# A hybrid decoder step on one core: gates and values projected 512 columns at a time, and the stores at the attention's ends issued by GpSimd

## The chip, the cores and the metric

The kernel runs on one core of one Trainium2 chip. The metric is the device time of one execution in microseconds (us); three runs of the kernel before gave a median of 3208.82 us, from 3206.28 to 3214.18. Engines are called as the profile calls them: PE (TensorE), PEld (its weight loads), DVE (VectorE), ACT (ScalarE), POOL (GpSimd) and SP (SyncE, which here only issues DMAs). Each engine works through its own instructions in order; an instruction that waits holds up everything behind it on that engine, DMA issues included.

## The reference, cut to what matters

One layer of a decoder with two kinds of heads, for one new sequence of 2048 tokens (the prompt) and 64 sampled tokens that attend to a paged cache. All is float32.

```python
z = einsum('bsd,dc->bsc', x, w_in)        # input projection, 1024 -> 3600 columns
fq, fk, fv, flogf = ...                   # 8 attention heads of 64: queries, keys, values, forget gates
mq, mk, mv, ig, lf = ...                  # 4 mLSTM heads of 128 (q and k through a short convolution)
og = sigmoid(z[..., OFF_M_O:] + b_og)     # output gate, 512 columns
fox_h = softmax(q k^T / 8 + decay, causal) v            # prompt attention, 2048 x 2048 per head
(C, n, m), m_h = scan of mLSTM chunks                   # states C_prompt, n_prompt are outputs
mn  = normalise(m_h) * mlstm_norm_w * og
x1  = layer_norm(ALPHA * x + concat(fox_h, mn) @ w_o)
y   = layer_norm(ALPHA * x1 + square(relu(x1 @ w1)) @ w2)
```

The sampled tokens take the same path, with attention over 8192 cached positions each.

## The kernel before, in words

Every large product is split: each float32 operand is taken as a high part (fp32r, made by ACT in `split_hi`, L153) and a rest (made by DVE in `split_lo`, L156), and `mm3` (L162 to L164) does three matmuls in place of one: high by high, and the two mixed ones.

**Phase A, the input projection**, goes over the prompt in four blocks of four 128-token tiles (block 1 has the sampled tokens as a fifth tile). `block_a` runs, for each block: the mLSTM values (two passes of 256 columns, the second with 16 gate columns), eight passes of 128 columns for the convolved q and k, two passes of 256 columns for the output gates, eight of 128 for queries and keys, and two of 256 for the attention's values, which are stored to `v_prompt`. In the passes of 128 columns the weights are the stationary operand and 512 tokens stream past. In the passes of 256 columns (`natural`) a token tile is stationary and 256 weight columns stream past: for each of the four tiles 8 row groups of 128 by 3 matmuls into one PSUM bank, then the pass's `sink` evacuates that bank. `wload` brings the weights of a pass in two pieces of 512 KB (four row groups by 256 columns, two raw buffers `wra`, four split ones `whi` and `wlo`).

Beside the projection run two other streams, a piece at a time: `tick` adds up microseconds and, whenever a pace is passed, issues one step of the mLSTM recurrence (`m_block`, one step per 2.3) or of the sampled tokens' attention (`sample_attention`, one step per 5.6). In `natural` a tick of 2.6 follows each tile. A step of the sampled attention has 32 small matmuls on gathered keys (`sQ`), or 16 on gathered values (`sO`); POOL issues the gathers (`kT`, `vt`). The sampled attention stops at a fixed step in phase A and goes on in later phases.

**Phase B**, the prompt's attention, is 64 units of (head, 256 queries), with the scores `pS` one unit ahead of the values `po`. Before a score leaves PSUM (DVE, L989 and L993), it needs the row of decays `nl` from DRAM and its masked last tile `nd`, which POOL makes (L974). At the end of each half of a head, `finish` scales the output `ot` by `rl` and stores it to the buffer `dmix` (L1061, L1062).

**Phase O** multiplies `dmix` by `w_o` (`pw`, with `mh`, `ml` from `dmix` and `wh`, `wl` from `w_o`, here in passes of 512 columns), and **phase C** is the MLP with one level of Strassen's scheme (`ph`, `py`).

The order of instructions on each engine is fixed when the program is built, by a scheduler that simulates the engines; the buffers (`bufs=`) limit how far ahead it may go.

Of the kernel before, what the change touches and what calls it, by code (L numbers as in the profile page):

```python
# [10 lines left out]
F32 = mybir.dt.float32  # L11
F32R = mybir.dt.float32r
I32 = mybir.dt.int32
AF = mybir.ActivationFunctionType
# [38 lines left out]
def body(ctx, tc, I, O, stages):  # L53
# [411 lines left out]
    def block_a(bi):  # L465
# [3 lines left out]
        def natural(sink, *cols, hook=None, after=None):  # L469
            wh, wl = W0.pop() if W0 else wload(*cols)  # L470
            for i, t in enumerate(blk):
# [9 lines left out]
                    after(i)  # L481
                tick(2.6)

        def stage(ps, m, n):
            st = pa.tile([128, 256], F32, name="st", bufs=4)[:m, :n]
            A.copy(st, ps)
            return st
# [68 lines left out]
        if bi == 3:  # L556
            SY.dma_start(O["conv_prompt"], hist)
        yield 1
        for i in range(2):
# [41 lines left out]
        for i in range(2):  # L601
            def sink(t, m, ps, i=i):
                d = v_out(t)[:, i * 256:(i + 1) * 256]
                (A if bi == 3 and i == 1 else SY).dma_start(d, stage(ps, m, 256))
# [9 lines left out]
            def b_first(n, i=i):  # L614
                if i == 1 and n == 0:
                    begin_b()
            natural(sink, (1024 + i * 256, 256), hook=b_first if bi == 3 else turn_first)

    dgs_s = drm.tile([4, 8], F32, name="dgs_s")

# [5 lines left out]
    def norm_out(hh, np_, og, tok0, eng=None):  # L626

        st = pm.tile([128, 4, 6], F32, name="st6", bufs=2)
        mv = pm.tile([128, 4, 2], F32, name="mv2", bufs=2)
        for h in range(4):  # L630
            V.bn_stats(st[:np_, h], hh[:, h])
            V.bn_aggr(mv[:np_, h], st[:np_, h])
        r = pm.tile([128, 2, 4], F32, name="r4", bufs=2)
        V.tensor_scalar(r[:np_, 0], mv[:np_, :, 1], EPS, None, op0=OP.add)
        G.tensor_tensor(r[:np_, 1], r[:np_, 0], nhalf[:np_, 0:4], op=OP.pow)
        for h in range(4):
            V.tensor_scalar(hh[:, h], hh[:, h], mv[:np_, h, 0:1], r[:np_, 1, h:h + 1], op0=OP.subtract, op1=OP.mult)
        hf = hh.rearrange("p h e -> p (h e)")
        (eng or G).tensor_tensor(hf, hf, og, op=OP.mult)

        def turn():
            po = ppm.tile([128, 4, 128], F32, name="mm", tag="mm", bufs=2)
            for h in range(4):
                T.transpose(po[:, h, :np_], hh[:, h], ident[:np_, :np_])
            ot = pm.tile([128, 4, 128], F32, name="ot", bufs=1)
            A.copy(ot[:, :, :np_], po[:, :, :np_])
            SY.dma_start(dmv[:, 4:8, tok0:tok0 + np_], ot[:, :, :np_])
        mst["turn"] = turn

    def turn_out():  # L650
# [28 lines left out]
    def m_block(bi):  # L679

        if bi == 0:
            mst["C"] = pm.tile([128, 4, 129], F32, name="Cs", bufs=2)
            V.memset(mst["C"], 0.0)
        gsb = pm.tile([128, 4, 4], F32, name="gsb", bufs=2)
        va, Wm, qa = m_load(bi * 4, mst["gates"])
        SY.dma_start(gsb, dap(dgs, bi * 4, [[0, 128], [16, 4], [1, 4]]))
        for _ in range(4):
            yield 1
        A.activation(gsb, gsb, AF.Exp)
        for c in range(bi * 4, bi * 4 + 4):  # L690
# [24 lines left out]
            pk = ppm.tile([128, 4, 128], F32, name="mm", tag="mm", bufs=2)  # L715
            for h in range(4):
                T.transpose(pk[:, h], qk[:, 4 + h], ident)
            kw = pm.tile([128, 4, 128], F32, name="kw", bufs=1)
            for h in range(4):
                V.tensor_scalar(kw[:, h], pk[:, h], wk[:, h:h + 1], KSC, op0=OP.mult, op1=OP.mult)  # L720
            hh = pm.tile([128, 4, 128], F32, name="hh", bufs=1)
            for p in range(2):
                yield 1
                pn = ppm.tile([128, 2, 129], F32, name="mn", tag="mm", bufs=2)
                for i in range(2):
                    h = 2 * p + i
                    T.matmul(pn[:, i], Wm[:, h], va[:, h], start=True, stop=False)
                    T.matmul(pn[:, i], qa[:, h], Cs[:, h], start=False, stop=True)
                h_out(pn, 2 * p, den[:, 2 * p:2 * p + 2], 128, hh)
            Cn = pm.tile([128, 4, 129], F32, name="Cs", bufs=2)  # L730
            va_ = va
            for p in range(2):
                yield 1
                pc = ppm.tile([128, 2, 129], F32, name="mn", tag="mm", bufs=2)
                for i in range(2):
                    T.matmul(pc[:, i], kw[:, 2 * p + i], va_[:, 2 * p + i], start=True, stop=True)
                for i in range(2):
                    h = 2 * p + i
                    V.scalar_tensor_tensor(Cn[:, h], Cs[:, h], gsb[:, h, c % 4:c % 4 + 1], pc[:, i], op0=OP.mult, op1=OP.add)
                if p == 0:  # L740
                    norm_out(hh, 128, og, t0, V if c == 15 else None)
                    if c % 4 < 3:
                        va, Wm, qa = m_load(c + 1)
            mst["C"] = Cn
        mst["open"] = False
        if bi < 3:
            return
        Cs = mst["C"]
        SY.dma_start(O["C_prompt"][0, 0].rearrange("h d e -> d h e"), Cs[:, :, 0:128])
        nn = pm.tile([128, 4], F32, name="nn", tag="sm", bufs=1)  # L750
        V.tensor_copy(nn, Cs[:, :, 128])
        SY.dma_start(O["n_prompt"], nn)
        yield 1
        turn_out()

# [148 lines left out]
    def phase_b():  # L904
# [95 lines left out]
        def values(z, g, sc):  # L1000
# [40 lines left out]
            A.copy(od, po[0:64])  # L1041
            q0 = 128 if g == 0 else 0
            V.tensor_tensor(od[:, q0:], od[:, q0:], po[64:128, q0:], op=OP.add)
            if g % 4 == 3:
# [2 lines left out]
        def finish(z, half):  # L1047
# [9 lines left out]
            for q in range(2):  # L1057
                rl = pb.tile([64, 512], F32, name="rl", bufs=2)
                SY.dma_start(rl, dap(drl, h * S + o + q * 512, [[0, 64], [1, 512]]))
                s = slice(q * 512, (q + 1) * 512)  # L1060
                G.tensor_tensor(ot[:, s], ot[:, s], rl, op=OP.mult)  # L1061
                SY.dma_start(dmix[h // 2, (h % 2) * 64:(h % 2) * 64 + 64, o + q * 512:o + q * 512 + 512], ot[:, s])  # L1062

        kns = [pb.tile([128, 512], F32, name="kn", bufs=3)]
        homes = {}
# [17 lines left out]
        for n in range(len(units) + LA):  # L1083
# [3 lines left out]
            while n and len(w2_done) < min(60 if False else 64, w2_due[0]):  # L1087
                w2_sum()
            if n == 60:
                wo.extend(half_wo(0, q) for q in range(4))  # L1090
            if n < len(units):
                h, g = units[n]
                sc[n] = scores(Z[h], g)
# [916 lines left out]
```

## Time and profile before

| | |
|---|---|
| median of three runs (lowest to highest) | 3208.82 us (3206.28 to 3214.18) |
| the profiled execution's own time | 3212.34 us |
| its span, first to last instruction | 3210.6 us |
| PE busy | 3115.6 us (97%) in 20445 matmuls |
| DVE / ACT / POOL busy | 2080.9 (65%) / 1442.2 (45%) / 902.6 us (28%) |
| mean granted TensorE clock | 0.989 |
| DMA | 732.67 MB, mean 228 GB/s |

Phase A ends at about 867 us of the span, phase B at about 1310, phase O at about 1545. A matmul's duration in the profile is its way through a pipeline: the next one starts before it ends. What a matmul costs a stream of matmuls is the distance from its start to the next one's start.

### The profile page before, as it was taken

To read this page: it belongs to the slowest core of one execution; us is meant where nothing else is said; L and a number is where in the kernel's file an instruction comes from. 1 tells how busy PE (TensorE), PEld (TensorE's weight loads), DVE (VectorE), ACT (ScalarE), POOL (GpSimd) and SP (SyncE) were. 2 spreads that over 40 slices of the span, in tenths; PEclk is the share of its full clock that TensorE was granted. 3 is DMA by queue.
4 is the path that set the end of the run, shared out by engine and by line. 5 is a ranking of instruction groups with operands and counts; after the bars stand their busy time and mean duration, and the time that the engine had idled before them with its cause. 6 is when DMAs were issued, how large, how long until landed. Compare 5 with 4: busy or idle time off the path is not lost. (4 is left out here: it accounts for less than half of the span.)

```text
span 3210.6 us, 55049 instructions
## 1 busy us (share of the span) xinstructions
PE 3115.6 (97%) x20445; PEld 2475.3 (77%) x20445; DVE 2080.9 (65%) x5046; ACT 1442.2 (45%) x2654; POOL 902.6 (28%) x973
## 2 busy tenths in 40 slices
PE   8999999999899999999999999999999999899998
PEld 8997797888767667777677777777767777698886
DVE  6957556465488788534557568556675665766667
ACT  3343343333277777412444445343444444344442
POOL 0121223423333333376333323334333111000000
PEclk9999999999999999999999999999999999999999
DMA  5565766866777865687887869878879866643231
GB/s 190 156 216 179 253 210 211 295 238 228 238 241 189 204 170 138 223 295 257 300 289 269 308 234 322 319 260 307 292 260 340 288 209 204 211 165 131 98 126 63
DMA packets 325075, 732.67 MB, mean 228 GB/s; under 512 B 63592, under 2 KB 161384, under 8 KB 323912
## 3 DMA queue, kind: packets, MB, share of 16 engines
q1 hardware_dynamic: 237672, 414.67, 39.8%
q0 software_dynamic: 83520, 304.12, 27.3%
q10 hardware_dynamic: 3616, 10.36, 0.9%
q8 instruction: 162, 2.65, 0.3%
q14 instruction: 105, 0.86, 0.1%
HBM read 676.20 MB, written 86.38 MB: 238 GB/s over the span
## 5 line engine op out<-in xcount | busy, mean ns | idle before, releaser
L156 DVE TENSOR_TENSOR wl<-wr,wh 128x1024 fp32r<-128x1024 f32 x300 | 365.9, 1223 | 244.0 <-ACT wh L153 204.8
L153 ACT ACTIVATE wh<-wr 128x1024 fp32r<-128x1024 f32 x300 | 315.3, 1055 | 332.0 <-PE py L164 123.7
L162 PE MATMUL ph<-x1h,wh 128*128 128x512 f32 (+1 forms) x1280 | 455.4, 356 | 0.0
L163 PE MATMUL ph<-x1l,wh 128*128 128x512 f32 (+1 forms) x1280 | 453.7, 355 | 0.2 <-DVE x1l L156 0.2
L164 PE MATMUL ph<-x1h,wl 128*128 128x512 f32 (+1 forms) x1280 | 451.7, 355 | 0.2
L1727 POOL DMA_INDIRECT kT<-cache_k,idxK x256 | 277.0, 1082 | 551.9 <-PE sQ L1750 483.2
L162 PE MATMUL py<-wh,hh 128*128 128x512 f32 x900 | 358.9, 403 | 10.1 <-issue 3.6
L163 PE MATMUL py<-wl,hh 128*128 128x512 f32 x900 | 354.5, 395 | 0.2 <-issue 0.2
L164 PE MATMUL py<-wh,hl 128*128 128x512 f32 x900 | 351.8, 395 | 0.4 <-DVE hl L156 0.4
L1376 DVE TENSOR_TENSOR y<-y,py 128x512 f32<-128x512 f32 x410 | 277.2, 683 | 108.4 <-PE py L164 83.0
L1838 POOL DMA_INDIRECT vt<-cache_v,idxV x164 | 178.9, 1091 | 401.4 <-PE sO L1862 341.5
L162 PEld LDWEIGHTS ph<-x1h,wh 128*128 128x128 f32 x1280 | 241.4, 189 | 40.6 <-issue 8.2
L164 PEld LDWEIGHTS ph<-x1h,wl 128*128 128x128 f32 x1280 | 240.8, 189 | 36.5 <-issue 3.7
L163 PEld LDWEIGHTS ph<-x1l,wh 128*128 128x128 f32 x1280 | 241.5, 189 | 34.9 <-issue 3.7
L162 PE MATMUL pm<-whi,xh 128*128 128x256 f32 (+2 forms) x816 | 238.2, 292 | 8.0 <-ACT whi L153 7.9
L163 PE MATMUL pm<-wlo,xh 128*128 128x256 f32 (+2 forms) x816 | 233.9, 287 | 1.0 <-DVE wlo L156 0.6
L164 PE MATMUL pm<-whi,xl 128*128 128x256 f32 (+2 forms) x816 | 234.1, 287 | 0.0
L162 PE MATMUL pm<-xh,whi 128*128 128x512 f32 (+2 forms) x640 | 230.5, 360 | 0.0
L164 PE MATMUL pm<-xh,wlo 128*128 128x512 f32 (+2 forms) x640 | 227.4, 355 | 0.0
L163 PE MATMUL pm<-xl,whi 128*128 128x512 f32 (+2 forms) x640 | 226.8, 354 | 0.0
L162 PEld LDWEIGHTS py<-wh,hh 128*128 128x128 f32 x900 | 169.3, 189 | 66.1 <-issue 25.8
L164 PEld LDWEIGHTS py<-wh,hl 128*128 128x128 f32 x900 | 170.7, 190 | 40.3 <-issue 2.3
(364 smaller groups left out, 6545.2 us busy)
## 6 DMA issues: line engine op xcount, KB each, us to landing
wr<-w SPq DMA_DIRECT2D x200, 512.0 KB
wra<-w_in SPq DMA_DIRECT2D x104, 512.0 KB
wr<-dw SPq DMA_DIRECT2D x96, 512.0 KB
dw<-w POOLq DMA_DIRECT2D x48, 512.0 KB
Rb<-dR SPq DMA_DIRECT2D x128, 128.0 KB
kT<-dw SPq DMA_DIRECT2D x28, 512.0 KB
kT<-w SPq DMA_DIRECT2D x25, 512.0 KB
xn<-xp_t SPq DMA_DIRECT2D x16, 512.0 KB
```

Source lines behind the costliest of these rows:

```text
L153: last["ACT"] = A.activation(dst, src, AF.Copy, scale=scale)
L156: r = (eng or V).tensor_tensor(dst, src, hi.bitcast(F32), op=OP.subtract)
L162: T.matmul(ps, wh, xh, start=first, stop=False, skip_group_check=shared)
L163: T.matmul(ps, wh, xl, start=False, stop=False, skip_group_check=shared)
L164: last["PE"] = T.matmul(ps, wl, xh, start=False, stop=stop, skip_group_check=shared)
L1376: V.tensor_tensor(y, y, ps, op=op)
L1727: G.indirect_dma_start(out=piece(n), out_offset=None, in_=ck, in_offset=IO(ap=idxK[:, b, j // 2, j % 2:j % 2 + 1], axis=0))
L1838: vx["last"] = G.indirect_dma_start(out=vt.rearrange("p f c -> p (f c)"), out_offset=None, in_=cv, in_offset=IO(ap=idxV[:, b, (kt % 4) * 4 ...
```

## The change

Three things change.

**Wider passes.** In blocks 2 to 4 the two passes of the output gates, and the two of the attention's values, become one pass of 512 columns each (`wide`). Four PSUM banks are open at once, one for each tile, and the weights come in four pieces of two row groups by 512 columns (still 512 KB, now read as two runs of 2 KB per partition in place of one of 4 KB). Each piece serves all four tiles before the next begins; a tile's bank is evacuated in the last piece, in one instruction where there were two, and stored in one DMA of 256 KB. The tick is 1.3 after each tile of each piece, and 1.23 for the sampled attention. The loads and the split of the next block's tokens hang on pieces of the values pass (`at`). Block 1 keeps its passes.

**Stores moved to GpSimd.** At the end of phase A, the last mLSTM tile's store to `dmix`, `C_prompt` and `n_prompt` are issued by POOL in place of SP. In block 4 all stores of the values are issued by ACT.

**The end of phase B.** For the last head's second half the scaling by `rl` goes from POOL to DVE and its stores from SP to POOL; the last unit's copy out of PSUM goes from ACT to DVE; and a fifth piece of `w_o` is loaded early.

```diff
+        def wide(sink, c0, hook=None):
+            banks = [ppa.tile([128, 512], F32, name="pm", tag="pm", bufs=4) for _ in blk]
+            at0, at1 = (w_at[((c0 + i * 256, 256),)] for i in range(2))
+            for q in range(4):
+                wr = pa.tile([128, 4 * 272], F32, name="wra", bufs=2)[:, :1024]
+                SY.dma_start(wr.rearrange("p (s e) -> p s e", s=2),
+                             dap(I["w_in"], at0 + q // 2 * 131072 + q % 2 * 512, [[1024, 128], [at1 - at0, 2], [1, 512]]))
...
+                split_hi(wh, wr)
+                split_lo(wl, wr, wh)
...
+                for i, t in enumerate(blk):
+                    xh, xl = xcol(bi, t)
+                    for k in range(2):
+                        mm3(banks[i].rearrange("p (s c) -> p s c", s=2), xh[:, 2 * q + k], xl[:, 2 * q + k], wh[:, k], wl[:, k],
+                            q == k == 0, q == 3 and k == 1)
+                    if hook:
+                        hook(q, i)
+                    if q == 3:
...
+                        sink(t, banks[i], st)
+                    tick(1.3, 1.23)
...
+        if bi:
+            wide(gate_out, C_O)
+        for i in range(0 if bi else 2):
...
+        def v_store(t, ps, st):
+            A.copy(st, ps)
+            (A if bi == 3 else SY).dma_start(v_out(t), st)
...
+        if bi:
+            wide(v_store, 1024, at)
+        for i in range(0 if bi else 2):
...
-            SY.dma_start(dmv[:, 4:8, tok0:tok0 + np_], ot[:, :, :np_])
+            (G if tok0 == S - 128 else SY).dma_start(dmv[:, 4:8, tok0:tok0 + np_], ot[:, :, :np_])
...
-        SY.dma_start(O["C_prompt"][0, 0].rearrange("h d e -> d h e"), Cs[:, :, 0:128])
+        G.dma_start(O["C_prompt"][0, 0].rearrange("h d e -> d h e"), Cs[:, :, 0:128])
...
-        SY.dma_start(O["n_prompt"], nn)
+        G.dma_start(O["n_prompt"], nn)
...
-            A.copy(od, po[0:64])
+            if (z["h"], g) == units[-1]:
+                V.tensor_copy(od, po[0:64])
+            else:
+                A.copy(od, po[0:64])
...
-                G.tensor_tensor(ot[:, s], ot[:, s], rl, op=OP.mult)
-                SY.dma_start(dmix[h // 2, (h % 2) * 64:(h % 2) * 64 + 64, o + q * 512:o + q * 512 + 512], ot[:, s])
+                end = (h, half) == (7, 1)
+                (V if end else G).tensor_tensor(ot[:, s], ot[:, s], rl, op=OP.mult)
+                (G if end else SY).dma_start(dmix[h // 2, (h % 2) * 64:(h % 2) * 64 + 64, o + q * 512:o + q * 512 + 512], ot[:, s])
...
-                wo.extend(half_wo(0, q) for q in range(4))
+                wo.extend(half_wo(*q) for q in ((0, 0), (0, 1), (0, 2), (0, 3), (1, 0)))
```

**Where instructions stand now.** Rows are `line operation out<-in size`, the line being that of each kernel's own source. First SP, at the passage from phase A to phase B, before the change: `Rb` is a load for the sampled attention, `nl0` the first decays of phase B, `vn0` and `kn` its values and keys.

```order
L647 DMA dmix_67<-ot_9777 128x4x128
L1734 DMA Rb_16283<-dR_69 128x1x256 x2
L749 DMA C_prompt<-Cs_9878 128x4x128
L752 DMA n_prompt<-nn_9970 128x4
L647 DMA dmix_67<-ot_9978 128x4x128
L932 DMA nl0_10000<-dnl_64 128x512
L933 DMA vn0_9999<-v_prompt 128x4x64
```

The same place on SP after the change.

```order
L226 DMA kn0_9072<-k_prompt 64x512
L226 DMA qn0_9073<-dq_60 64x256
L694 DMA dmix_67<-ot_9089 128x4x128
L979 DMA nl0_9304<-dnl_64 128x512
L980 DMA vn0_9303<-v_prompt 128x4x64
```

The load of `nl0` no longer stands behind the three last stores of the mLSTM, but behind the store of the last tile but one. POOL at the same passage before the change: `vt` are the two halves of a gather of cached values, `dmask` the causal mask.

```order
L635 TENSOR_TENSOR r4_9956<-r4_9956,nhalf_74 128x4
L1838 DMA vt_9909<-cache_v,idxV_1539 128x1024
L1838 DMA vt_9911<-cache_v,idxV_1539 128x1024
L926 MEMSET ls_10007 128x32
L926 MEMSET ls_10197 128x32
L1078 AFFINE_SELECT dmask_10009<-dmask_10009 128x128
L974 TENSOR_TENSOR nd_10021<-nl0_10000,dmask_10009 128x128
```

POOL at the same passage after the change.

```order
L682 TENSOR_TENSOR r4_9208<-r4_9208,nhalf_74 128x4
L796 DMA C_prompt<-Cs_9174 128x4x128
L799 DMA n_prompt<-nn_9240 128x4
L973 MEMSET ls_9311 128x32
L973 MEMSET ls_9501 128x32
L1889 DMA vt_9281<-cache_v,idxV_1539 128x1024
L1129 AFFINE_SELECT dmask_9313<-dmask_9313 128x128
L694 DMA dmix_67<-ot_9248 128x4x128
L1889 DMA vt_9283<-cache_v,idxV_1539 128x1024
L1021 TENSOR_TENSOR nd_9325<-nl0_9304,dmask_9313 128x128
```

Three stores and the two halves of the gather now stand ahead of the first `nd`. PE at that passage before the change: `mn` and `mm` belong to the last mLSTM tile, `pm` is the projection, `pS` the first score of phase B.

```order
L163 MATMUL pm_9913<-wlo_9735,xh_146 128x256
L164 MATMUL pm_9913<-whi_9734,xl_147 128x256
L736 MATMUL mn_9941<-va_9619,kw_9785 128x129 x2
L736 MATMUL mn_9964<-va_9619,kw_9785 128x129 x2
L644 MATMUL mm_9973<-ident_73,hh_9790 128x128 x4
L981 MATMUL pS_10023<-ks0_10001,qh_10002 128x256
```

PE there after the change.

```order
L163 MATMUL pm_8895<-wlo_9151,xh_146 128x512
L783 MATMUL mn_9193<-va_8990,kw_9097 128x129 x2
L164 MATMUL pm_8895<-whi_9150,xl_147 128x512
L783 MATMUL mn_9234<-va_8990,kw_9097 128x129 x2
L1801 MATMUL sQ_9251<-kT_2647,qb_8304 32x256 x16
L691 MATMUL mm_9243<-ident_73,hh_9102 128x128 x4
L1913 MATMUL sO_8577<-vt_9140,PTs_9128 32x256 x4
L1913 MATMUL sO_8577<-vt_9138,PTs_9128 32x256 x4
L1028 MATMUL pS_9327<-ks0_9305,qh_9306 128x256
```

The last step of the sampled attention (`sQ` and `sO`) stood ahead of the last tile's projection; it now stands behind it, around the mLSTM's last transposes `mm`. Last, DVE at the passage from phase B to phase O before the change: `po` is the last unit's product, `ot` its copy.

```order
L1031 COPY PT_16146<-pt_16153 128x4x128
L1043 TENSOR_TENSOR ot_15877<-ot_15877,po_16119 64x256
L84 MEMSET pad_5x_16245 128x1
L156 TENSOR_TENSOR ml_16226<-xr_16223,mh_16225 128x1024
L156 TENSOR_TENSOR wl_16230<-wr_15669,wh_16229 128x1024
```

DVE there after the change.

```order
L1078 COPY PT_15452<-pt_15459 128x4x128
L1112 TENSOR_TENSOR ot_15183<-ot_15183,rl_15503 64x512
L1089 COPY ot_15183<-po_15425 64x256
L1093 TENSOR_TENSOR ot_15183<-ot_15183,po_15425 64x256
L1112 TENSOR_TENSOR ot_15183<-ot_15183,rl_15507 64x512
L84 MEMSET pad_5x_15551 128x1
L156 TENSOR_TENSOR ml_15532<-xr_15529,mh_15531 128x1024
L156 TENSOR_TENSOR wl_15536<-wr_14973,wh_15535 128x1024
```

Two multiplications and the copy have come in ahead of the first split of phase O on DVE; on ACT the copy is gone, and `mh` and `wh` stand directly behind the last copies of transposed scores.

More of the change, by code (lines that the diff above doesn't have):

```diff
@@ L482, in natural @@
                 tick(2.6)
+        def wide(sink, c0, hook=None):
[5 more added lines that the diff above has]
+                             dap(I["w_in"], at0 + q // 2 * 131072 + q % 2 * 512, [[1024, 128], [at1 - at0, 2], [1, 512]]))
+                wh = pa.tile([128, 4 * 272], F32R, name="whi", bufs=4)[:, :1024]
+                wl = pa.tile([128, 4 * 272], F32R, name="wlo", bufs=4)[:, :1024]
+                split_hi(wh, wr)
+                split_lo(wl, wr, wh)
+                wh, wl = (x.rearrange("p (s k c) -> p k s c", s=2, k=2) for x in (wh, wl))
+                for i, t in enumerate(blk):
[6 more added lines that the diff above has]
+                    if q == 3:
+                        st = (pa.tile([128, 512], F32, name="sa", tag="ac", bufs=2) if i % 2 else
+                              pa.tile([128, 512], F32, name="sq", tag="qi", bufs=2))
+                        sink(t, banks[i], st)
+                    tick(1.3, 1.23)
         def stage(ps, m, n):
@@ L558, in block_a, with gate_out @@
         yield 1
-        for i in range(2):
+        def gate_out(t, ps, st):
+            V.tensor_tensor(st, ps, bog, op=OP.add)
+            A.activation(st, st, AF.Tanh, scale=0.5)
+            V.scalar_tensor_tensor(st, st, 1.0, nwh, op0=OP.add, op1=OP.mult)
+            SY.dma_start(dog[t * 128:t * 128 + 128], st)
+        if bi:
+            wide(gate_out, C_O)
+        for i in range(0 if bi else 2):
             def sink(t, m, ps, i=i):
@@ L600, in block_a, with at @@
         kx["new"] = True
-        for i in range(2):
+        def v_store(t, ps, st):
+            A.copy(st, ps)
+            (A if bi == 3 else SY).dma_start(v_out(t), st)
+        def at(q, i):
+            if bi == 3:
+                if (q, i) == (2, 0):
+                    begin_b()
+            elif q < 3 and i == 0:
+                x_load(BLKS[bi + 1][q])
+            elif (q, i) == (3, 0):
+                x_turn(bi + 1, BLKS[bi + 1][0])
+                x_load(BLKS[bi + 1][3])
+        if bi:
+            wide(v_store, 1024, at)
+        for i in range(0 if bi else 2):
             def sink(t, m, ps, i=i):
-                d = v_out(t)[:, i * 256:(i + 1) * 256]
-                (A if bi == 3 and i == 1 else SY).dma_start(d, stage(ps, m, 256))
+                SY.dma_start(v_out(t)[:, i * 256:(i + 1) * 256], stage(ps, m, 256))
             def turn_first(n, i=i):
@@ L612, in turn_first @@
                     x_load(BLKS[bi + 1][3])
[L614 to L617, printed above, removed]
+            natural(sink, (1024 + i * 256, 256), hook=turn_first)
     dgs_s = drm.tile([4, 8], F32, name="dgs_s")
```

## The prediction

> **What bounds the kernel now.** I read the page's busy times first, then the waits of PE, then one of the passes that the change rewrites. On the page, the span and the busy times:
>
> ```profile
> span 3210.6 us, 55049 instructions
> PE 3115.6 (97%) x20445; PEld 2475.3 (77%) x20445; DVE 2080.9 (65%) x5046; ACT 1442.2 (45%) x2654; POOL 902.6 (28%) x973
> ```
>
> PE is busy 97% of the span, so a change must shorten PE's stream or fill its holes; DVE and ACT have room. The profiled execution took 3212.34 us, 3.5 above the median of the runs, 3208.82. I make the sum against the first and then take it off the median. A measurement of this kernel can tell about 0.3%, 9.6 us, from no change. Where PE does wait (engine and line, what it waited for, us in total, times, longest):
>
> ```profile
> PE sO L1862 <- DMA vt<-cache_v,idxV: 18.3, 6, 6.2
> PE pt L1026 <- ACT S L1010: 10.5, 3, 7.4
> PE pm L162 <- ACT whi L153: 7.9, 1, 7.9
> ```
>
> Two things are to be seen. The projection waited for a weight piece only once, before its first matmul, so weights are not what its passes wait for. And one wait of 7.4 us, in front of a transpose of phase B, is the largest hole that a part of this change touches. The two values passes of block 4, as a stretch (start:end, length, then busy time of each engine, granted clock, DMA share and GB/s):
>
> ```profile
> 832.00:865.50 33.50, 33.50 (x315) 31.41 (x315) 12.77 (x58) 8.26 (x25) 14.23 (x15) 1.00 0.65 208
> ```
>
> PE is busy throughout, at full clock. These passes are bound by PE's own stream.
>
> **Wider passes.** What they remove is counted in the groups by shape:
>
> ```profile
> L162 PE MATMUL pm<-whi,xh 128*128 128x256 f32 x640 | 186.8, 292 | 0.0
> L164 PE MATMUL pm<-whi,xl 128*128 128x256 f32 x640 | 183.2, 286 | 0.0
> L163 PE MATMUL pm<-wlo,xh 128*128 128x256 f32 x640 | 183.0, 286 | 0.5 <-issue 0.5
> ```
>
> 640 each are 5 passes x 16 tiles x 8 row groups. The change touches 4 passes x 12 tiles x 8 = 384 of each line, 1152 in all, and makes 576 of 512 columns of them. The mean durations here, near 290 ns, are ways through the pipeline and must not be multiplied. The distance from start to start is in PE's timeline, first and last of eight matmuls of 256 columns in a row, then of eight of 512:
>
> ```profile
> 857.70 0.28 PE L163 MATMUL pm<-wlo,xh 128*128 128x256 f32 x1
> ...
> 858.54 0.28 PE L164 MATMUL pm<-whi,xl 128*128 128x256 f32 x1
> 395.10 0.39 PE L163 MATMUL pm<-xl,whi 128*128 128x512 f32 x1
> ...
> 396.70 0.40 PE L164 MATMUL pm<-xh,wlo 128*128 128x512 f32 x1
> ```
>
> (858.54 - 857.70) / 7 = 0.120 us, and (396.70 - 395.10) / 7 = 0.2286 us. Two narrow ones cost 0.240, one wide 0.2286: 0.0114 saved, and 576 x 0.0114 = **6.6 us**, all of it on PE's stream. A rule speaks against most of this: by the Trainium skill, "TensorE: Matmul & The Clock Gate", section "Back-to-back issue gap", the isolated spacing is the columns over 2.4 GHz plus 2.5 ns, thus 109 and 216 ns, and an estimate by it saves 2.5 ns a pair, 1.4 us in all. The rows above differ from it: the part that does not grow with the columns is nearer to 11 ns, and I go by the rows.
>
> The rest of this part costs PE nothing. Evacuations halve in number (24 DVE pairs with a tanh, and 24 ACT copies, for 48 each) and are bunched into the last piece; a bank is needed again only after the three other tiles' matmuls of that piece, 18 x 0.2286 = 4.1 us. If that cover were gone, one 512-column evacuation per pass would show, some 0.7 us by the 0.42 us that a 256-column one takes further down, six times. A weight piece is now used up in (33.5 - 1.1) / 4 = 8.1 us where two were used up in 16.8, so the need for pieces is the same per microsecond, with more pieces split ahead; each now arrives in runs of 2 KB in place of 4. No row shows 2 KB runs of this size; I take no cost, and price the other case below. The ticks: the recurrence gets 16 x 1.3 = 20.8 as before, the sampled attention 16 x 1.23 = 19.7, thus 1.1 less in each of six passes, 6.7 / 5.6 = 1.2 steps. This is why its last step slides behind the projection.
>
> **The passage from A to B.** First the last gathers and the last step in time order, with an earlier pair of steps, then the passage (start, duration, engine, operation; in brackets the idle time before and what ended it):
>
> ```profile
> 800.53 1.05 PE L1862 MATMUL sO<-vt,PTs 128*32 128x256 f32 x16
> 811.14 0.64 PE L1862 MATMUL sO<-vt,PTs 128*32 128x256 f32 x8 [1.64 <-DMA vt<-cache_v,idxV]
> 861.40 1.05 PE L1862 MATMUL sO<-vt,PTs 128*32 128x256 f32 x16
> 863.11 1.07 POOL L1838 DMA_INDIRECT vt<-cache_v,idxV  x1 [0.19 <-issue]
> 864.49 1.27 POOL L1838 DMA_INDIRECT vt<-cache_v,idxV  x1 [0.30 <-issue]
> 866.65 0.66 PE L644 MATMUL mm<-ident,hh 128*128 128x128 f32 x4 [0.25 <-DVE Cs L739]
> 867.34 0.59 ACT L646 COPY ot<-mm 128x512 f32<-128x512 f32 x1 [1.43 <-PE mm L644]
> 868.43 0.63 SPq L647 DMA_DIRECT2D dmix<-ot  x1
> 869.12 0.68 SPq L932 DMA_DIRECT2D nl<-dnl  x1
> 869.54 0.58 PE L981 MATMUL pS<-ks,qh 128*128 128x256 f32 x1 [2.23 <-DVE ks L156]
> 876.53 1.69 POOL L974 TENSOR_TENSOR nd<-nl,dmask 128x128 f32<-128x128 f32 x4 [8.70 <-DMA nl<-dnl]
> 877.02 0.29 DVE L993 CUSTOM_DVE_ANT_0 S<-pS,nd 128x128 f32<-128x128 f32 x1 [7.54 <-POOL nd L974]
> ```
>
> Let T be the start of the last transposes, 866.65. SP is held by the store of `ot` until ACT has copied it, issues it at 868.43 and only then `nl`, which lands 7.4 us later, at 876.53. DVE's first score stands at T + 10.4. With the stores off SP, `nl` goes out one mLSTM tile earlier and has landed by T. What ends last is then POOL's row: the first half of the gather waits until PE has used half of the last `sO`, T + 0.66 + 0.53 = T + 1.2, and issues in 1.07; the mask, as small as `nd`, takes 1.69 / 4 = 0.42; then the store of `ot`, for which ACT is done at T + 1.3. How long POOL takes to issue a plain store no row shows: between SP's 0.63 and the gather's 1.27, I take 1.1, as it is POOL that does it. The second half of the gather takes 1.27, `nd` 0.42. That is T + 1.2 + 1.07 + 0.42 + 1.1 + 1.27 + 0.42 = T + 5.5, and DVE follows at T + 5.6: **4.8 us** earlier. The new wait is POOL's for `ot`; behind it are that half gather, which nobody needs before phase O, and `nd`, which DVE needs and PE behind DVE. T itself moves by two things that I let cancel: 1.05 us of `sO` now fill the hole behind T, and the transposes may wait about as long, as fewer projection matmuls stand between them and the products they come from. The bounds are 0, where the gather of the last `sO` comes late (10.6 us passed between the two steps at 800.53 and 811.14 when PE waited for it, and the order leaves about as much), and the whole wait of 7.5.
>
> **The passage from B to O.**
>
> ```profile
> 1305.88 3.67 PE L1036 MATMUL po<-PT,vn 128*64 128x256 f32 x32
> 1307.28 1.26 POOL L1061 TENSOR_TENSOR ot<-ot,rl 64x512 f32<-64x512 f32 x1 [23.25 <-DMA rl<-drl]
> 1309.60 0.37 ACT L1041 COPY ot<-po 64x256 f32<-64x256 f32 x1 [3.03 <-PE po L1036]
> 1309.87 1.05 ACT L153 ACTIVATE mh<-xr 128x1024 fp32r<-128x1024 f32 x1
> 1310.00 0.42 DVE L1043 TENSOR_TENSOR ot<-ot,po 64x256 f32<-64x256 f32 x1 [4.30 <-ACT ot L1041]
> 1310.83 3.89 ACT L153 ACTIVATE wh<-wr 128x1024 fp32r<-128x1024 f32 x4
> 1310.96 1.90 DVE L156 TENSOR_TENSOR ml<-xr,mh 128x1024 fp32r<-128x1024 f32 x1 [0.53 <-ACT mh L153]
> 1311.92 0.50 PE L162 MATMUL pw<-wh,mh 128*128 128x512 f32 x1 [2.38 <-ACT wh L153]
> 1312.78 4.62 DVE L156 TENSOR_TENSOR wl<-wr,wh 128x1024 fp32r<-128x1024 f32 x4
> 1314.05 0.80 PE L163 MATMUL pw<-wl,mh 128*128 128x512 f32 x1 [1.62 <-DVE wl L156]
> 1317.32 1.21 DVE L156 TENSOR_TENSOR ml<-xr,mh 128x1024 fp32r<-128x1024 f32 x1
> ```
>
> PE loses 2.38 + 1.62 = 4.0 us here. With the copy off ACT, `mh` and `wh` are made before the last `po` ends at 1309.55, and the first wait goes. The second does not: DVE now copies (0.42) and adds (0.42) and multiplies 64x512 (half of the 1.21 for 128x1024, 0.6) from 1309.60 on, thus until 1311.05; then `ml` takes 1.21, its price where POOL is not multiplying beside it, and `wl` 4.62 / 4 = 1.16, until 1313.4. PE goes on at 1313.5 in place of 1314.05: **0.5 us**. The first multiplication is DVE's new wait, for `rl`, which landed by 1307.28, with the copy, `ml` and `wl` queued behind; it is over before `po` ends. POOL's two stores wait for DVE, and the gathers of phase O queue behind them, some 2 us later than now; nobody waits for those at once. The fifth piece of `w_o` and the freed SP hide behind the 8 x 3 matmuls of the first unit. Bounds: a loss of 0.5 if the copy is dearer on DVE, a gain of 4.0.
>
> The sum is 6.6 + 4.8 + 0.5 = 11.9 us: 3212.34 - 11.9 = 3200.4 for the profiled execution, and on the median 3208.82 - 11.9 = **3197 us**.
>
> **The rivals.** *The half clock goes too.* At both passages the granted clock is low:
>
> ```profile
> 868.00:884.00 16.00, 6.36 (x19) 3.65 (x19) 5.93 (x26) 4.05 (x12) 2.60 (x6) 0.57 0.86 238
> 1313.20:1320.00 6.80, 5.96 (x14) 4.70 (x15) 6.47 (x6) 3.40 (x4) 2.49 (x2) 0.50 1.00 335
> ```
>
> In the second, PE works 6.8 us at half speed, and at full clock would need 3.4 less. In the first it is busy only 6.36 us, of which up to 2.7 would go. If the holes become short enough, 3.4 + 2.7 = 6.1 us come on top: 3191. For it: both low stretches begin just behind a hole. Against it: at 1309.55 PE still stands for 4 us but for one matmul. The Trainium skill, "TensorE: Matmul & The Clock Gate", section "What's actually happening", puts the halving down to an idle window of about 3.4 us; that agrees with the second stretch, and leaves it open whether 4 us of idleness hold such a window.
>
> *The wide passes save nothing.* If a matmul's cost goes with its columns alone, or the `sO` waits (18.3 us) take up what the matmuls leave because gathers keep their own time, only 5.3 us remain: 3203.5. For it: the gather at 811.14 came 1.64 us late. Against it: the steps stay as far apart, 33.5 x 5.6 / 20.8 = 9.0 us before and 32.4 x 5.6 / 19.7 = 9.2 after. By the skill's formula above it would be 3202.
>
> *Slower: weight pieces come late.* SP is in order, and it stands long for free raw buffers:
>
> ```profile
> SPq L283 <- DVE wlo L156: 88.3, 37, 9.4
> ```
>
> The 24 wide pieces must each be loaded, split by ACT and by DVE within 8.1 us, behind stores that wait. A piece that comes 1 us late stops PE four tiles long at once: 24 us lost, 3197 + 24 = 3221. It turns the sign beyond 0.3% from (11.9 + 9.6) / 24 = 0.9 us a piece. Against it stands the single wait for `whi` above; for it, that ACT and DVE have bunched evacuations in just the piece before the next pass.
>
> **How the numbers follow.** The forecast has 0.55, of which 0.45 beyond 0.3% and 0.10 within, as 11.9 is little over 9.6; the half clock 0.17, all faster; no saving 0.20, within; late pieces 0.08. So faster 0.62, same 0.30, slower 0.08. The range runs from 3186, the half clock's 3191 with 5 us for waits that fall elsewhere in a reordered phase A, to 3209, the unsaved case with the same 5 us; late pieces are left out.
>
> **What would show it.** Right: 576 matmuls of 512 columns at 0.229 us from start to start; `nl` landed before the last `mm`; the first `nd` about 5.5 us behind T, with POOL's own row as what came before it; the first `pw` directly behind `po` and the second near 4 us later. Wrong: waits of `pm` for `whi` or `wlo`, more than 18.3 us of `sO` waits, or a first score more than 10 us behind T.

## The result and the profile after

The changed kernel took 3194.98 us (median of 10 runs, 3187.10 to 3203.64) against 3208.48 for the kernel before (10 runs, 3205.06 to 3216.66): a ratio of 0.9959, 95% interval 0.9947 to 0.9970, thus 13.5 us less where 11.9 were forecast. The profiled execution took 3198.31 us. On its page, the busy times:

```profile
PE 3103.8 (97%) x19869; PEld 2442.8 (76%) x19869; DVE 2081.3 (65%) x5025; ACT 1439.5 (45%) x2629; POOL 907.0 (28%) x976
```

576 matmuls fewer, as counted. The groups by shape have 192 matmuls of 512 columns on each of the three lines, and in PE's timeline two of them stand seven places apart:

```profile
L162 PE MATMUL pm<-whi,xh 128*128 128x512 f32 x192 | 77.2, 403 | 0.0
```

```profile
845.16 0.39 PE L163 MATMUL pm<-wlo,xh 128*128 128x512 f32 x1
...
846.75 0.39 PE L164 MATMUL pm<-whi,xl 128*128 128x512 f32 x1
```

(846.75 - 845.16) / 7 = 0.227 us. The waits of PE that the prediction named (what for, us in total, times, longest):

```profile
PE sO L1913 <- DMA vt<-cache_v,idxV: 14.7, 7, 5.6
PE pm L162 <- ACT whi L153: 7.9, 1, 7.9
PE pt L1073 <- ACT S L1057: 5.0, 2, 3.6
```

No new wait for a weight piece; the wait for `S` in front of phase B's first transposes is 5.0 where it was 10.5, and the wait of `pw` for `wh` is no longer there. Not all waits fell: that of phase B's transposes for the copies `PT` is 9.7 here where it was 5.9, but 5.2 in a second profile of the changed kernel (experiment 4), so no saving or loss can be read from it.

**The passage from A to B**, in time order:

```profile
853.47 0.51 SPq L979 DMA_DIRECT2D nl<-dnl  x1
864.30 0.33 SPq L979 DMA_DIRECT2D nl<-dnl  x1
866.66 3.51 SPq L1003 DMA_DIRECT2D qn<-dq  x4
866.70 0.66 PE L691 MATMUL mm<-ident,hh 128*128 128x128 f32 x4
869.55 0.81 POOL L694 DMA_DIRECT2D dmix<-ot  x1
870.66 1.00 POOL L1889 DMA_INDIRECT vt<-cache_v,idxV  x1 [0.30 <-issue]
871.69 2.09 POOL L1021 TENSOR_TENSOR nd<-nl,dmask 128x128 f32<-128x128 f32 x5
872.19 0.29 DVE L1040 CUSTOM_DVE_ANT_0 S<-pS,nd 128x128 f32<-128x128 f32 x1 [3.20 <-POOL nd L1021]
873.35 0.48 PE L1073 MATMUL pt<-ident,S 128*128 128x128 f32 x1 [3.58 <-ACT S L1057]
```

T is 866.70. The first decays left SP 13.2 us before it; the row at 864.30 is the second load, of the decays for the next queries, and 866.66 is the load of those queries, `qn`. POOL's own row is what ends last, and the first score stands at 872.19, T + 5.5 (forecast T + 5.6). Five `nd` now follow each other; before, four did, and the fifth came later.

**The passage from B to O:**

```profile
1304.39 3.67 PE L1083 MATMUL po<-PT,vn 128*64 128x256 f32 x32
1307.99 0.50 PE L162 MATMUL pw<-wh,mh 128*128 128x512 f32 x1
1308.11 0.42 DVE L1089 COPY ot<-po 64x256 f32<-64x256 f32 x1 [1.72 <-PE po L1083]
1309.64 1.21 DVE L156 TENSOR_TENSOR ml<-xr,mh 128x1024 fp32r<-128x1024 f32 x1
1312.04 0.50 PE L163 MATMUL pw<-wl,mh 128*128 128x512 f32 x1 [3.55 <-DVE wl L156]
```

From the end of `po` (1308.06) to the second `pw` it is 3.98 us; before, it was 1314.05 - 1309.55 = 4.50. The gain is 0.52.

**What two single profiles would have told.** Set side by side, the two executions put almost the whole gain where nothing was changed. Phase C from its first `ph` to the end of its first half (start:end, length, busy times, granted clock, DMA share, GB/s), of the kernel before, then of the changed one:

```profile
1537.00:2770.70 1233.70, 1209.54 (x7425) 905.98 (x7426) 782.90 (x1414) 543.55 (x838) 373.89 (x356) 0.99 0.79 279
```

```profile
1534.50:2755.30 1220.80, 1200.88 (x7425) 903.68 (x7426) 785.07 (x1414) 546.16 (x838) 377.15 (x356) 1.00 0.79 282
```

12.9 us less with the same 7425 matmuls in the same order. And phase A from block 2's first 512-column matmul to T, where 6.6 us were forecast, shows hardly a gain, 614.65 before and 614.20 after:

```profile
252.00:866.65 614.65, 605.96 (x4382) 508.73 (x4379) 361.44 (x1034) 226.01 (x473) 185.96 (x197) 0.99 0.70 232
```

```profile
252.50:866.70 614.20, 602.89 (x3789) 478.01 (x3787) 359.79 (x1004) 222.27 (x451) 183.49 (x195) 0.99 0.69 233
```

The experiments were made to tell which of this is the change and which is the execution.

### The profile page after: what moved, and what is told of

Read it like the earlier page. It is cut to its first block, busy times and chain, and to the rows that moved or that the text cites. A ratio compares the mean times of both kernels' runs of the same rounds, so it can differ in the third digit from the quotient of the medians.

```text
span 3196.6 us, 53750 instructions
## 1 busy us (share of the span) xinstructions
PE 3103.8 (97%) x19869; PEld 2442.8 (76%) x19869; DVE 2081.3 (65%) x5025; ACT 1439.5 (45%) x2629; POOL 907.0 (28%) x976
## 4 chain that ended last, share of the span: by engine, by line
PE 47%; DMA 4%; DVE 1%; issue 1%; POOL 1%; ACT 0%; DVEq 0%; POOLq 0%; ACTq 0%
PE ph L162 7%; PE ph L164 7%; PE ph L163 7%; PE py L162 6%; PE py L163 6%; PE py L164 6%; PE sO L1913 3%; DMA vt<-cache_v,idxV 2%; PE sQ L1801 2%; PE ph L169 1%; PE sT L1870 1%; DMA kT<-cache_k,idxK 1%; DMA xr<-cache_v,idxV 0%; DVE wl L156 0%; PE pw L163 0%
## 5 line engine op out<-in xcount | busy, mean ns | idle before, releaser
L162 PE MATMUL pm<-whi,xh 128*128 128x256 f32 (+4 forms) x624 | 202.3, 325 | 7.9 <-ACT whi L153 7.9
L156 DVE TENSOR_TENSOR wlo<-wra,whi 128x1024 fp32r<-128x1024 f32 (+1 forms) x112 | 140.8, 1258 | 102.7 <-ACT whi L153 102.3
L163 PE MATMUL pm<-wlo,xh 128*128 128x256 f32 (+4 forms) x624 | 200.4, 321 | 0.6 <-DVE wlo L156 0.6
L164 PE MATMUL pm<-whi,xl 128*128 128x256 f32 (+4 forms) x624 | 199.9, 321 | 0.6 <-DVE xl L156 0.6
```

Of the source, the lines that this page charges most:

```text
L156: r = (eng or V).tensor_tensor(dst, src, hi.bitcast(F32), op=OP.subtract)
L162: T.matmul(ps, wh, xh, start=first, stop=False, skip_group_check=shared)
L163: T.matmul(ps, wh, xl, start=False, stop=False, skip_group_check=shared)
L164: last["PE"] = T.matmul(ps, wl, xh, start=False, stop=stop, skip_group_check=shared)
```

## The experiments

Each kernel was timed in five rounds beside the kernel before; kernels of one group of four ran on one chip. Intervals are 95%.

**1. The wide passes alone** (the changed kernel without its other two parts):

```diff
-            (G if tok0 == S - 128 else SY).dma_start(dmv[...], ot[...])
+            SY.dma_start(dmv[...], ot[...])          # C_prompt, n_prompt likewise
...                                                   # copy on A, scaling on G, stores on SY, four pieces of w_o
```

> The wide passes alone; the stores at the attention's ends and the end of phase B as before. Theory of the sum (each part saves what the prediction gave it): 6.6 us less than before, ratio 0.998, with the gain inside phase A: the mLSTM's last transposes start near 860 of the span and not 866.7. Rival from the two traces (phase A gives the saving back in holes and half-clock stretches, since T was 866.65 before and 866.70 after): T stays near 866.7 and the ratio lies within 0.999 to 1.001.

Measured: 0.9981 (0.9972 to 0.9990), 3198.28 us. T stands at 861.50, and block 2 to T takes 609.00 us:

```profile
252.50:861.50 609.00, 598.54 (x3790) 474.62 (x3787) 358.52 (x1004) 222.37 (x451) 182.72 (x195) 1.00 0.69 234
```

PE's matmuls up to T are here the same, in the same order, as in the changed kernel. So the changed kernel's 614.20 was the longest that this order took (605.8 to 614.2 in eight executions, see below), and the rival falls by the ratio, whose interval ends at its lower bound. The passage holds the surprise:

```profile
861.36 0.44 SPq L979 DMA_DIRECT2D nl<-dnl  x1
861.50 0.66 PE L691 MATMUL mm<-ident,hh 128*128 128x128 f32 x4
862.96 0.53 SPq L694 DMA_DIRECT2D dmix<-ot  x1
866.60 1.69 POOL L1021 TENSOR_TENSOR nd<-nl,dmask 128x128 f32<-128x128 f32 x4 [1.11 <-DMA nl<-dnl]
867.08 0.29 DVE L1040 CUSTOM_DVE_ANT_0 S<-pS,nd 128x128 f32<-128x128 f32 x1 [3.30 <-POOL nd L1021]
872.87 0.45 POOL L1021 TENSOR_TENSOR nd<-nl,dmask 128x128 f32<-128x128 f32 x1 [4.58 <-DMA nl<-dnl]
```

The first score stands at T + 5.6 although all three stores are still issued by SP: with the wide passes the scheduler puts the decays ahead of the store of `ot`. Only the fifth `nd`, for the next queries, is late, T + 11.4.

**2. The three stores alone**, on the kernel before:

```diff
-            SY.dma_start(dmv[...], ot[...])
+            (G if tok0 == S - 128 else SY).dma_start(dmv[...], ot[...])   # C_prompt, n_prompt: G
```

> Only the three stores at the end of phase A moved from SP to GpSimd, everything else as before. Theory of the sum: 4.8 us less, ratio 0.9985; first masked score at T + 5.6 instead of T + 10.4, first transpose of phase B at T + 6.7 instead of T + 11.4. Rival (phase B takes the time back in its own waits for scores and copies, since B as a whole became only 3.4 us shorter in the changed kernel): the score comes as early, but the first matmul of phase O stays at about T + 445 and the ratio is within 0.0005 of 1.

Measured: 1.0009 (0.9999 to 1.0019). The score comes early and nothing follows:

```profile
865.24 0.66 PE L644 MATMUL mm<-ident,hh 128*128 128x128 f32 x4 [0.26 <-DVE Cs L739]
871.23 0.29 DVE L993 CUSTOM_DVE_ANT_0 S<-pS,nd 128x128 f32<-128x128 f32 x1 [3.14 <-POOL nd L974]
875.78 0.63 ACT L153 ACTIVATE ks<-kn 128x512 fp32r<-128x512 f32 x1 [8.44 <-DMA kn<-k_prompt]
876.32 0.39 ACT L1010 ACTIVATE S<-S,mx 128x128 f32<-128x128 f32 x1
876.85 1.18 PE L1026 MATMUL pt<-ident,S 128*128 128x128 f32 x3 [7.97 <-ACT S L1010]
```

The score is at T + 6.0, but ACT, in order, stands 8.44 us before the split of the next keys `kn`, and the exponential that PE waits for is queued behind it. The first transpose is at T + 11.6; before, it was at T + 11.5, and the first matmul of phase O stays at T + 445.8. One wait has taken the other's place: the rival. Its upper bound, 1.0005, lies inside the interval, the theory's 0.9985 does not.

**3. The end of phase B alone**, on the kernel before:

```diff
-            A.copy(od, po[0:64])
+            (V.tensor_copy if (z["h"], g) == units[-1] else A.copy)(od, po[0:64])   # written as if and else
...                                     # scaling on V, stores on G, fifth piece of w_o
```

> Only the end of phase B changed: copy and scaling on DVE, stores on GpSimd, fifth piece of w_o. Theory of the sum: 0.5 us less, not to be told from 1.000; PE's wait for wh gone, its second wait near 4 us. Rival (the passage is worth the 2 us that lie between the second matmuls of phase O in the two traces, and gathers of phase O come later and cost some of it): ratio 0.9995 or above 1.0005.

Measured: 0.9992 (0.9979 to 1.0004); the waits as forecast, the second `pw` 0.5 us earlier behind the last `po`. In time it cannot be told from nothing.

**4. The changed kernel again.**

> The changed kernel once more, unaltered, as a measure of what one execution's profile says. Both theories: ratio 0.996. Theory of chance: the 13 us by which phase C (first ph to the first matmul of line 169 behind the first MLP half) was shorter in the changed kernel, with PE's instructions in the same order, are half-clock stretches and holes of that one execution; here the stretch comes out anywhere between 1221 and 1234 us. Rival (the change causes it, by another order on GpSimd): 1221 again, within 3 us.

Measured: 0.9961 (0.9948 to 0.9973). Phase C's first half took 1227.1 us, halfway between the two. In other executions, with the same order of matmuls, it was 1221.4 (experiment 1) and 1235.2 us (experiment 12) with the wide passes, and 1225.8 (experiment 3) and 1226.4 us (experiment 8) without them. The 12.9 us between the first two profiles were chance. Block 2 to T took 610.7, the first score was at T + 5.5, the fifth `nd` at T + 6.6 again.

**5. The wide passes and the stores** (experiment 1 with the three stores on GpSimd).

> The wide passes and the three stores on GpSimd; the end of phase B as before. Theory now (the wide passes alone already bring the decays to the front of SP's queue, so the stores have nothing left to give): ratio as with the wide passes alone, 0.9975 to 0.9985, first masked score at T + 5.5. Rival (the stores cost by themselves, as alone: 1.0009): 0.999. Rival (the stores pay only together with the wide passes, since the changed kernel stands 0.002 below the wide passes alone): 0.9965.

Measured: 0.9953 (0.9939 to 0.9967), nearest to the rival that they pay together.

**6. The wide passes and the end of phase B** (experiment 1 with that edit).

> The wide passes and the changed end of phase B; the three stores on SP as before. Theory now (the parts add, 0.9981 and 0.9992): 0.9973, PE's wait for wh gone. Rival (the end of phase B gives only the 0.5 us of the prediction): 0.998. Rival (this pair is all of the change): 0.996.

Measured: 0.9977 (0.9966 to 0.9988), not to be told from the wide passes alone; the rival that this pair is all of the change, 0.996, is outside.

Where the stores pay is seen in the 50 us behind T. PE's waits for ACT there, in the changed kernel, then with the wide passes alone:

```profile
PE pt L1073 <- ACT S L1057: 5.0, 2, 3.6
```

```profile
PE pt L1073 <- ACT S L1057: 6.1, 2, 3.7
PE pS L1028 <- ACT qh L153: 5.2, 2, 4.1
```

and the matmuls `po` done in these 50 us (PE busy with them and their count in the first place, then PEld, DVE and ACT; the granted clock of the stretch in the third place from the end), of before, of the changed kernel, of the wide passes alone:

```profile
866.65:916.65 50.00, 7.81 (x56) 3.67 (x56) 1.56 (x4) 1.43 (x4) 0.83 0.70 205
```

```profile
866.70:916.70 50.00, 11.87 (x76) 5.37 (x76) 1.98 (x5) 1.80 (x5) 0.90 0.78 236
```

```profile
861.50:911.50 50.00, 10.08 (x60) 4.47 (x60) 1.56 (x4) 1.45 (x4) 0.80 0.75 215
```

Three executions with wide passes and stores (the changed kernel twice, experiment 5) have 76 each and a clock of 0.90; three with the wide passes and the stores on SP (experiments 1, 6 and 12) have 60 each and 0.80 to 0.83. PE's wait for `qh` (3.5 to 5.2 us in those three) goes with the stores. The stores on GpSimd do not bring this by themselves, in any order: the kernels of experiments 7 and 11 have them too, and 60 `po` at a clock of 0.86. PE's wait for `qh` comes from ACT. Its longest in experiment 1, with what ACT itself had waited for, the queries `qn`, and SP's issue of them:

```profile
865.31 3.40 SPq L1003 DMA_DIRECT2D qn<-dq  x4
874.66 0.88 ACT L153 ACTIVATE qh<-qn 128x256 fp32r<-128x256 f32 x2 [3.17 <-DMA qn<-dq]
875.13 1.54 PE L1028 MATMUL pS<-ks,qh 128*128 128x384 f32 x3 [4.05 <-ACT qh L153]
```

SP began to issue these queries at T + 3.8, behind the stores and the second decays; in the changed kernel it began at T. The keys come late too. What ACT waited for `kn` in the same 50 us, in the changed kernel, then with the wide passes alone:

```profile
ACT ks L153 <- DMA kn<-k_prompt: 0.2, 1, 0.2
```

```profile
ACT ks L153 <- DMA kn<-k_prompt: 6.2, 5, 2.9
```

**7. Halves**: the changed kernel with two matmuls of 256 columns in place of each wide one.

```diff
-                    for k in range(2):
-                        mm3(banks[i].rearrange("p (s c) -> p s c", s=2), xh[:, 2 * q + k], xl[:, 2 * q + k], wh[:, k], wl[:, k], ...)
+                    for s in range(2):
+                        for k in range(2):
+                            mm3(banks[i][:, s * 256:s * 256 + 256], xh[:, 2 * q + k], xl[:, 2 * q + k], wh[:, k, s], wl[:, k, s], ...)
```

> The changed kernel with each wide matmul issued as two of 256 columns, 1152 in place of 576; pieces, banks, evacuations, loads and stores as in the changed kernel. Theory (the wide matmul itself saves 0.0114 us a pair): 6.6 us slower than the changed kernel, ratio to before 0.998. Rival (the saving comes from the order and the pieces, not from the matmul's width): as the changed kernel, 0.996.

Measured: 0.9984 (0.9973 to 0.9996), as the theory has it. Against the changed kernel's 0.9959 and 0.9961 that is 0.0024 more, 7.7 us; the half widths of the two intervals, 0.0012 each, make some 0.0017 of uncertainty, thus 2 to 13 us. But more than the width differs: the scheduler gives this kernel another order, with the sampled attention's last step wholly behind T, the first score at T + 7.4 and 60 `po` in the 50 us behind T. Block 2 to T, of this kernel, then of experiment 10 (wide matmuls, the same clock):

```profile
251.60:858.13 606.53, 601.03 (x4332) 504.40 (x4330) 361.30 (x1001) 221.77 (x448) 187.14 (x193) 1.00 0.71 236
253.00:858.83 605.83, 596.90 (x3789) 473.32 (x3786) 360.45 (x1004) 222.33 (x451) 185.46 (x195) 1.00 0.70 236
```

The narrow matmuls keep PE busy 4.1 us longer, 6.1 with the 1.93 us of `sQ` that have gone behind T, near the forecast. Yet the stage is only 0.7 us longer (2.6 with that `sQ`), as PE stands idle 5.5 us in it in place of 8.9. So these two traces show the work that the width saves, and also that about half of it comes back as waits; how the 7.7 us divide between the width and the order stays open.

**8. The pace alone**, on the kernel before:

```diff
-                tick(2.6)
+                tick(2.6, 2.46 if bi and cols[0][0] in (C_O, C_O + 256, 1024, 1280) else None)
```

> The kernel before with nothing but the pace changed: the sampled attention gets 2.46 instead of 2.6 behind each tile of the gates and values passes of blocks 2 to 4, as the wide passes give it 16 x 1.23. Theory (moving the last step behind the projection is what frees the decays' load on SP): first masked score at about T + 5.6, ratio 0.999. Rival (it is the wide passes' own bunching): T + 10, ratio 0.9995 to 1.0005.

Measured: 1.0024 (1.0012 to 1.0036), slower by about 7.7 us, which neither expected. In this order SP issues the store of `ot` and two loads of `w_o` ahead of the decays:

```profile
870.74 0.66 PE L644 MATMUL mm<-ident,hh 128*128 128x128 f32 x4 [2.16 <-DVE hh L639]
872.04 0.37 SPq L647 DMA_DIRECT2D dmix<-ot  x1
872.50 0.95 SPq L1145 DMA_DIRECT2D wr<-w_o  x2
873.50 0.44 SPq L932 DMA_DIRECT2D nl<-dnl  x1
882.40 0.29 DVE L993 CUSTOM_DVE_ANT_0 S<-pS,nd 128x128 f32<-128x128 f32 x1 [5.28 <-POOL nd L974]
```

The first score comes at T + 11.7. So the step's move behind the projection does not by itself bring the decays forward.

**9 to 12.** Four more on one chip: the wide passes with the stores on ACT (`A.dma_start` for the three), with only `C_prompt` and `n_prompt` on GpSimd, with the stores on GpSimd and `tick(1.3)` for both streams, and the wide passes alone again.

> As the wide passes with the three stores, but the stores issued by ACT in place of GpSimd. Theory now (what pays is that SP's loads of phase B are no longer behind the stores; the engine that issues them does not matter): ratio as with GpSimd, 0.995 to 0.9965, and the fifth nd directly behind the first four, near T + 6.6. Rival (ACT is in order and waits for its own copy; a store ahead of the first splits delays them): first masked score later than T + 7, ratio 0.998.

> The wide passes with only C_prompt and n_prompt on GpSimd; the store of ot to dmix stays on SP, between the two halves of the second load of keys. Theory now: the first decays go out early, the second stand behind the store of ot, which waits for ACT until about T + 1.3, so the fifth nd comes near T + 10 and most of the stores' gain is gone: ratio 0.9975. Rival (the two state stores were what held SP): the fifth nd at T + 6.6, ratio 0.9955.

> The wide passes and the three stores, with the ticks back at the old pace: 1.3 for both streams, so that the sampled attention's last step of phase A stands where it stood before. Theory (the pace does not matter by itself): 0.9955. Rival (with the old pace the step's work comes back in front of the projection's end, and T is 1 to 2 us later): 0.9965. Rival (the new pace costs, as alone: 1.0024): 0.993.

> The wide passes alone a second time, on the same chip as the three others, to hold against the stores. Theory now: 0.998, fifth nd near T + 11 and 13 us of half clock behind T, as in the first execution. Rival (the first comparison was chance): 0.996, fifth nd near T + 6.6.

Measured, stores on ACT: 0.9968 (0.9954 to 0.9981), an interval that holds the upper part of the theory's range and the rival's 0.998. The first score is at T + 4.5 and the fifth `nd` at T + 5.7, as the theory has it; but ACT waited 6.6 us for `kn` in the 50 us behind T (0.7 in experiment 5), and `po` came to 60. Early decays alone do not carry the gain; the keys and the queries have to be early too. In experiment 5 SP issued the second keys at T - 12.2; here it stood 11.1 us in front of them, by the profile until stores of values had landed, issued them from T - 4.7 on, and the queries from T + 2.8. Why it stands there, with SP's loads in the order of experiment 5, stays open.

Only the state stores: 0.9962 (0.9949 to 0.9974), fifth `nd` at T + 8.8, again 60 `po`; the ratio lies between the two expectations, with the rival's 0.9955 inside its interval and the theory's 0.9975 just outside.

The old pace: 0.9953 (0.9937 to 0.9969), as its first theory has it, though by another road: T is at 856.57 and the 50 us behind it hold 60 `po`. The first rival's 0.9965 is inside the interval too, the second's 0.993 is not.

The wide passes alone again: 0.9961 (0.9948 to 0.9975), where 0.9981 had been measured: the ratio of the rival, but with the fifth `nd` at T + 10.5 as before. One and the same kernel thus gave two ratios 0.0020 apart on two chips, so what the stores add to the wide passes (0.9953, 0.9959 and 0.9961 with them; 0.9961, 0.9977 and 0.9981 without) is likely by the runs and not certain, about 5 us between the means. In the traces it shows in the 50 us behind T. From T to the second `pw` it took 445.3, 438.7 and 441.6 us with wide passes and stores (the changed kernel twice, experiment 5), 447.9, 442.5 and 449.4 with the stores on SP (experiments 1, 6 and 12): the same way, with a scatter as large as the difference.

## Why the prediction was right, and where its reasons were not

- **Wider matmuls, 6.6 us: right as PE's work, only in part as time.** The spacing fell from 0.240 for two to 0.227, or 0.013 x 576 = 7.5 us of PE's stream, and the wide passes alone are faster in both measurements (0.9981 and 0.9961). The wide passes' weights were waited for nowhere; the rival of late pieces didn't occur. What the prediction left out is that the stage has waits that grow when PE's work shrinks (experiment 7, and the point on T below), so "all of it on PE's stream" did not become all of it in time; putting the halves back cost 7.7 us (2 to 13), but with another order. The formula of the Trainium skill ("TensorE: Matmul & The Clock Gate", section "Back-to-back issue gap") for an isolated matmul saves 1.4 us by the prediction's estimate, about a fifth of what the spacing in these rows gives.
- **The passage from A to B, 4.8 us: the size was right, the edit was not.** T + 5.5 came with POOL's row as its last step. That it came to 0.1 us is luck in part: the issue of the store of `ot` took 0.81 in place of the estimated 1.1 and the gather's second half 1.00 in place of 1.27, and the first half began at T + 1.5 in place of T + 1.2. But the step "With the stores off SP, `nl` goes out one mLSTM tile earlier" holds for the changed kernel only as one of two sufficient ways: the wide passes' order alone gives T + 4.5 to 5.6, and the stores alone give T + 6.0 and no time, since ACT then waits 8.4 us for `kn`. The prediction followed the chain to DVE's score and stopped; one more step, to ACT's in-order queue and the loads of keys and queries that it waits for, was what is late next. What the stores do bring, with the wide passes, is behind the first score: the fifth `nd` at T + 6.6 instead of T + 10.3 to 11.4, the wait for `kn` down to 0.2 us and PE's wait for `qh` gone.
- **The passage from B to O, 0.5 us: right** to 0.02 us in the trace; too small for the runs.
- **T in the profile: the forecast gain of 6.6 us in front of it wasn't there**, by chance of one execution and since part of it is lost. In eight executions with the changed kernel's order of matmuls up to T (its first profile and experiments 1, 4, 5, 6, 9, 10 and 12) block 2 to T took 605.8 to 614.2 us, 609.5 in the mean; in three with the order of before (its profile, experiments 2 and 3) 612.5 to 614.7, 613.9 in the mean. That is 4.4 us, of which 1.05 is the `sO` now behind T, so some 3.4 of the 6.6 are left. Part of the saving is given back there: the changed order has waits of its own in phase A, 3.3 us for `PTs` and 2.6 for `ot`, as the wait for values falls from 5.1 to 1.2 (kernel before, then changed, up to 866 us):

```profile
PE sO L1862 <- DMA vt<-cache_v,idxV: 5.1, 3, 2.6
```

```profile
PE sT L1928 <- ACT PTs L1872: 3.3, 1, 3.3
PE mm L764 <- ACT ot L693: 2.6, 1, 2.6
PE sO L1913 <- DMA vt<-cache_v,idxV: 1.2, 1, 1.2
```

- **The half clock** went in part behind T, as the first rival had it: 0.83 to 0.90 in those 50 us, 50 x 0.07 = 3.5 us of full clock, which count where PE is busy (41 of the 50 us). In the profile of the changed kernel the low stretches that went here stand elsewhere again, in phases A and B: the mean granted clock is 0.989 in both profiles, and the rival's 6 us do not show in it.

That the total of 13.5 us is close to the sum of 11.9 is therefore luck in part. Of the largest term the work is confirmed and about half is seen as time in its stage, the smallest is confirmed in the trace, and the middle one belongs to two edits together and not to the one that it was given to, with a value that the runs leave uncertain. Whether the wide passes and stores without the end of phase B (0.9953) are better than the changed kernel (0.9959, 0.9961) these runs cannot say.

## What to carry to other kernels

Where a scheduler writes the order, an edit far away can move the very load that another edit was made for: try each part alone before a gain is put down to it. Following a freed wait means going on along every in-order queue up to the engine that sets the time, not only to the instruction that waited. And a single pair of profiles can place 13 us in a phase where nothing changed; before reading a stage, look at the same stage in a second execution of the same kernel.

## What the runs showed of the hardware

With 7425 matmuls in one fixed order, the same stretch of phase C took from 1220.8 to 1235.2 us from one execution to the next, about 1%, with the mean granted clock between 0.99 and 1.00 and hardly a change of load, 279 to 282 GB/s. A small load that SP issued at the passage took 5 to 7 us to reach POOL: `nl` of experiment 1 was issued at 861.36 and POOL had it at 866.60, 5.2 us later, with a DMA share of 0.84 from 861 to 867; in the kernel before it took 7.4 us (869.12 to 876.53), with a share of 0.99 from 867 to 873.
